# Low halves of the weights made by adding DMAs instead of the vector engine, in a two-layer decoder kernel

## The chip, the cores and the metric

The kernel runs on one core of a Trainium2 chip. The metric is the device time of one launch in microseconds. The engines are named as in the profile: PE multiplies matrices, PEld loads its weights, DVE is the vector engine, ACT the scalar engine, POOL is GpSimd, and SP issues DMAs.

## The reference

The program is one inference step of a trunk with two layers. 512 new prompt tokens and 8 x 4 sample tokens (544 in all, width 1024) go through it with the same weights:

```python
for l in range(DEPTH):                       # DEPTH = 2
    h = rms_norm(x, norm1_w[l])
    z = h @ w_in[l]                          # 1024 -> 3584: q, k, v, gate of retention; q, k, v of attention
    x = x + concat(retention(z), dilated_attention(z)) @ w_out[l]     # 1024 -> 1024
    h = rms_norm(x, norm2_w[l])
    u = h @ w_up[l]                          # 1024 -> 5632
    c = causal_depthwise_conv3(u)            # with a bias
    x = x + (silu(c[:, :2816]) * c[:, 2816:]) @ w_down[l]             # 2816 -> 1024
y = rms_norm(x, final_norm_w)
```

The sample tokens attend to 1024 cached positions and carry a retention state and a convolution buffer; the new keys, values, states and buffers are outputs too. All data are float32.

## The kernel before, in words

**Products in three passes.** A float32 product is made of three products of the PE's faster float32r type. Each operand is split into a high half (the operand rounded to float32r) and a low half (the operand minus its high half). `products` (lines 1368 to 1374) adds up high x high, high x low and low x high in that order; the third pass is the first that reads the weight's low half. The 544 tokens are two column groups of 272, so one 128 x 128 piece of a weight costs six matmuls.

**Blocks and units.** `main` is the list of output blocks in the order of the work: per layer 28 of `w_in`, 16 of `w_out` (four row pieces each), 44 of `w_up`, and 16 of `w_down`. Their weights come in units (`halves`), mostly 512 KB (128 partitions x 1024 numbers, 48 matmuls); the last eight blocks of `w_down` have units of 256 KB (24 matmuls). `load_w` (line 321) issues a unit's load on SP's queue into `raw`. `split_w` (line 335) lets ACT write the high half `wh` from `raw`, and spawns a piece of work that lets DVE write the low half `wl` = `raw` - `wh`. `raw`, `wh` and `wl` have three buffers each (`UNITS`). In the main loop (lines 1400 to 1419) the load of unit s+3 is issued at the start of unit s, and unit s+2 is split in the middle of unit s.

**What sets the order.** The program is written out once, by hand and by a planner: `Clock` (line 66) keeps a modelled time for every engine, for one DMA queue and for every tile; `Engine.charge` adds the modelled cost of each instruction. Between the matmuls of the main blocks `Stream.pump` takes up waiting pieces (attention, retention, evacuations, convolutions, splits), when their inputs are ready by the model; `st.before` does so while the PE would wait for an operand. So each engine has one fixed queue, and an instruction that waits holds up all behind it.

**Stages of a layer.** The `w_in` blocks run with attention and retention woven in; then `w_out`; then `w_up`, with convolution, gating and (class `Weave`) most of `w_down` woven in as a seven-product scheme, whose sums of weights (`sums`) and of activations (`fa`, `fb`) POOL makes; then the rest of `w_down`, which ends in the last eight blocks of 24 matmuls. After each of these eight, ACT and DVE prepare the next norm (`xh`, `sq`, `xl`). POOL issues no DMA in this kernel.

Of the kernel before, what the change touches and what calls it, by code (L numbers as in the profile page):

```python
# [9 lines left out]
F32 = mybir.dt.float32  # L10
F32R = mybir.dt.float32r
AF = mybir.ActivationFunctionType
OP = mybir.AluOpType
# [8 lines left out]
KB = D // 128  # L22
# [24 lines left out]
NCONV = 352  # L47
EARLY = 640
UNITS = 3


SEM = {"pe": 0.22, "act": 0.2, "dve": 0.14, "pool": 0.08, "sp": 0.1}
# [2 lines left out]
def need(kind, *aps, banks=0):  # L55
    return kind, aps, banks


def free_size(ap):
    n = 1  # L60
    for d in ap.shape[1:]:
        n *= d
    return n
# [36 lines left out]
class Engine:  # L100
# [20 lines left out]
    def charge(self, method, outs, ins, args, kw):  # L121
        c, kind = self.clock, self.kind
        n = free_size(outs[0]) if outs else 0
        if method == "dma_start":
            c.now["sp"] = max(c.now["sp"], c.when("sp", ins)) + 0.06
            c.dma = max(c.dma, c.now["sp"] + 0.8) + n * outs[0].shape[0] * 4 / 3.6e5
            c.wrote[c.key(outs[0])] = ("sp", c.dma + 1.0)
            return
        if kind == "pe":
            rows = outs[0].shape[0]  # L130
            if method == "transpose":
                cost = max(n, 128) * 2 / 2400
            elif (kw["lhsT"]).dtype == F32R:
                cost = max(n / 2400, 0.107)
            else:
                side = min(rows, kw["lhsT"].shape[0])
                cost = max(n * 4 / 2400, 0.21) / (1 if side > 64 else 128 // side)
            cost += 0.003
        elif kind == "act":
            ptr = sum(free_size(i) == 1 for i in ins[1:])  # L140
            cost = 1.3 if method.startswith("preload") else n / 1200 + 0.093 * (1 + ptr)
        elif kind == "dve":
            half = method in ("tensor_scalar", "tensor_copy")
            cost = (n * (0.5 if half else 1) + 66 + (60 if len(ins) > 2 else 0)) / 960
        else:
            cost = 0.1 + n * (2.2 if len(ins) > 1 else 1.0) / 1000
        c.issue(kind, outs, ins, cost)
# [84 lines left out]
def trunk(ctx: ExitStack, tc: tile.TileContext, xin, w_in, w_out, w_up, w_down, q_down, kc, vc, s0, sctx_d, params_d,  # L232
# [3 lines left out]
    pe, act, dve, pool, sp = (Engine(clock, k, e) for k, e in (  # L236
        ("pe", nc.tensor), ("act", nc.scalar), ("dve", nc.vector), ("pool", nc.gpsimd), ("sp", nc.sync)))
# [7 lines left out]
    st = Stream(clock, SHARE)  # L245
    uid = [0]

    def name(s):
        uid[0] += 1
        return f"{s}_{uid[0]}"  # L250

    def blk(shape, dt=F32, s="b"):
        return work.tile(shape, dt, name=name(s), tag="blk", bufs=NBLK)
# [8 lines left out]
    def EW(eng, *aps):  # L262
        return need(eng, *aps)
# [20 lines left out]
    def rotate(t, tag, bufs):  # L284
        ends = rot.setdefault(tag, [])
        if len(ends) >= bufs:
            old = clock.key(ends[len(ends) - bufs])
            last = max(clock.used.get(old, ("pe", 0.0)), clock.wrote.get(old, ("pe", 0.0)), key=lambda v: v[1])
            clock.used[clock.key(t)] = last
        ends.append(t)  # L290
        return t
# [12 lines left out]
    main = []  # L304
    halves = []
# [12 lines left out]

    raw, split = {}, {}

    def load_w(s):
        if s < len(halves):
            i, a, b = halves[s]
            if s < 4:
                raw[s] = blk([128, b - a, 128], F32, "raw")
            else:
                raw[s] = rotate(wpool.tile([128, b - a, 128], F32, name=name("raw"), tag="raw", bufs=UNITS), "raw",
                                UNITS)
            if main[i]["count"] > 1:
                sp.dma_start(raw[s].rearrange("p (n k) c -> p n k c", n=main[i]["count"]),  # L330
                             main[i]["src"].rearrange("n p k c -> p n k c"))
            else:
                sp.dma_start(raw[s], main[i]["src"][:, a:b, :])

    def split_w(s, at_once=False):
        if s < len(halves):
            i, a, b = halves[s]
            if s < 4 or i >= len(main) - KB:
                hi, lo = (blk([128, b - a, 128], F32R, n) for n in ("wh", "wl"))
            else:  # L340
                hi, lo = (rotate(wpool.tile([128, b - a, 128], F32R, name=name(n), tag=n, bufs=UNITS), n, UNITS)
                          for n in ("wh", "wl"))
            w = raw.pop(s)
            act.activation(hi, w, AF.Copy)

            def rest():
                dve.tensor_sub(lo, w, hi.bitcast(F32))
                split[s] = (hi, lo)
                return
                yield  # L350
            if at_once:
                list(rest())
            else:
                st.spawn(rest(), "split", EW("dve", hi))

# [976 lines left out]
    for l in range(DEPTH):  # L1332
        mixer(l)
        ffn(l)


    first = norms[0][0]
    act.preload_act_table_set("natural_log_exp_and_others")
# [11 lines left out]
    for what, n in start:  # L1350
        if what == "x":
            sp.dma_start(x[n], xin[:, n])
        else:
            load_w(n)
    load_w(4)
    for what, n in start:
        if what == "x":
            list(first.scale(n))
            if n < 4:
                list(first.square(n, pool))  # L1360
        else:
            split_w(n, True)
# [17 lines left out]
    for k in range(KB):  # L1380
        if k == 2:
            load_w(5)
        if k == 4:
            split_w(4)
            load_w(6)
        if k == 6:
            split_w(5)
        for n in range(2):
            s = 2 * n + k // 4
            products(main[n], ps[n], k, parts_of(s), k // 4 * 4)  # L1390
            if k % 4 == 3:
                split.pop(s)
            if k == KB - 1:
                main[n]["evac"](ps[n])
                ps[n] = None
            st.pump(0.7)
# [3 lines left out]
    for i, b in enumerate(main[2:-KB]):  # L1400
# [4 lines left out]
        for pi, (a, e) in enumerate(b["parts"]):  # L1405
            s = b["first"] + pi
            at, count = b["at"], b["count"]
# [16 lines left out]
    for c in range(2):  # L1424
        for n, b in enumerate(main[-KB:]):
            s, nk = b["first"], b["nk"]
# [145 lines left out]
```

## Time and profile before

| | before |
|---|---|
| median of three runs | 1441.15 us (1440.74 to 1441.16) |
| profiled execution | 1442.15 us, its span 1440.4 us |
| PE busy | 1404.5 us, 98% of the span |
| PEld busy | 1331.5 us, 92% |
| DVE busy | 1066.9 us, 74% |
| ACT busy | 582.4 us, 40% |
| POOL busy | 411.8 us, 29% |
| DMA, share of 16 engines | 34.4% by SP's queue, 172.01 MB |

Busy time is time in which an engine executed something. A PE that is 98% busy is not at its peak everywhere, since matmuls overlap in its pipeline; the number of matmuls in a stretch says more. A wait says what ended an engine's idle time. Every operation goes through one helper, so all lines are L118, and the tiles' names tell the operations apart.

### The profile page before, as it was taken

To read this page: it belongs to the slowest core of one execution; us is meant where nothing else is said; L and a number is where in the kernel's file an instruction comes from. 1 tells how busy PE (TensorE), PEld (TensorE's weight loads), DVE (VectorE), ACT (ScalarE), POOL (GpSimd) and SP (SyncE) were. 2 spreads that over 40 slices of the span, in tenths; PEclk is the share of its full clock that TensorE was granted. 3 is DMA by queue.
4 is the path that set the end of the run, shared out by engine and by line. 5 is a ranking of instruction groups with operands and counts; after the bars stand their busy time and mean duration, and the time that the engine had idled before them with its cause. 6 is when DMAs were issued, how large, how long until landed. Compare 5 with 4: busy or idle time off the path is not lost.

```text
span 1440.4 us, 28487 instructions
## 1 busy us (share of the span) xinstructions
PE 1404.5 (98%) x11442; PEld 1331.5 (92%) x11442; DVE 1066.9 (74%) x1911; ACT 582.4 (40%) x986; POOL 411.8 (29%) x745
## 2 busy tenths in 40 slices
PE   8999999999999999999999999999999999999997
PEld 8888888999999999999997888799999999999996
DVE  8767545687888888887777764455978797979775
ACT  4344323444434343433524442333544343434334
POOL 4312222002334454530021221110024353535303
PEclk9999999999999999999999999999999999999999
DMA  6214683433322222222332238732433222222222
GB/s 237 98 60 155 249 299 118 139 115 126 103 88 95 83 103 76 101 75 67 109 110 83 89 142 289 283 129 91 147 111 101 77 103 89 89 89 89 74 63 85
DMA packets 70821, 173.84 MB, mean 121 GB/s; under 512 B 7584, under 2 KB 11808, under 8 KB 70688
## 3 DMA queue, kind: packets, MB, share of 16 engines
q1 hardware_dynamic: 70688, 172.01, 34.4%
q8 instruction: 90, 1.47, 0.4%
q14 instruction: 43, 0.35, 0.1%
HBM read 159.77 MB, written 12.21 MB: 119 GB/s over the span
## 4 chain that ended last, share of the span: by engine, by line
PE 74%; DVE 16%; POOL 4%; issue 3%; ACT 2%; DMA 1%; SPq 0%; DVEq 0%; ACTq 0%; POOLq 0%
PE ps L118 52%; PE sec L118 22%; DVE p L118 3%; DVE rb L118 3%; DVE c L118 2%; DVE wl L118 2%; DVE y L118 1%; POOL sums L118 1%; POOL fb L118 1%; DVE u L118 1%; POOL fa L118 1%; ACT c L118 1%; DVE x L118 1%; DVE ra L118 1%; DVE fl L118 1%
## 5 line engine op out<-in xcount | busy, mean ns | idle before, releaser
L118 PE MATMUL ps<-xh,wh 128*128 128x272 f32 x2304 | 488.7, 293 | 1.9 <-ACT wh L118 1.6
L118 PE MATMUL ps<-xh,wl 128*128 128x272 f32 x2304 | 476.6, 288 | 1.4 <-DVE wl L118 1.3
L118 PE MATMUL ps<-xl,wh 128*128 128x272 f32 x2304 | 476.9, 288 | 0.0
L118 PEld LDWEIGHTS ps<-xh,wh 128*128 128x128 f32 x2304 | 360.2, 189 | 19.9 <-issue 15.5
L118 PEld LDWEIGHTS ps<-xh,wl 128*128 128x128 f32 x2304 | 361.7, 188 | 1.8 <-DVE wl L118 1.8
L118 PEld LDWEIGHTS ps<-xl,wh 128*128 128x128 f32 x2304 | 361.7, 188 | 0.1
L118 DVE TENSOR_TENSOR wl<-raw,wh 128x1024 fp32r<-128x1024 f32 (+1 forms) x182 | 220.3, 1211 | 14.8 <-ACT wh L118 13.5
L118 ACT ACTIVATE wh<-raw 128x1024 fp32r<-128x1024 f32 (+1 forms) x182 | 182.0, 1001 | 67.8 <-PE ps L118 59.0
L118 ACT ACTIVATE c<-u,taps 128x560 f32<-128x560 f32 x88 | 75.4, 857 | 279.5 <-DVE u L118 197.3
L118 DVE SCALAR_TENSOR_TENSOR c<-u,taps,c 128x560 f32<-128x560 f32 x176 | 150.6, 855 | 47.9 <-ACT c L118 44.2
L118 POOL COPY last<-u 128x2 f32<-128x2 f32 (+1 forms) x176 | 50.2, 317 | 344.3 <-DVE u L118 336.4
L118 DVE TENSOR_TENSOR x<-x,sec 128x272 f32<-128x272 f32 (+1 forms) x224 | 105.1, 472 | 44.0 <-PE sec L118 42.5
L118 POOL TENSOR_TENSOR sums<-uraw 128x256 f32<-128x256 f32 x64 | 69.1, 1080 | 84.7 <-DVE sl L118 84.6
L118 DVE TENSOR_TENSOR u<-ps,rstd 128x512 f32<-128x512 f32 (+1 forms) x176 | 68.9, 432 | 13.1 <-PE ps L118 12.7
L118 DVE TENSOR_TENSOR rb<-ps,rope 32x544 f32<-32x544 f32 (+1 forms) x96 | 69.2, 721 | 1.4
L118 DVE TENSOR_TENSOR x<-x,ps 128x544 f32<-128x544 f32 (+1 forms) x72 | 46.9, 654 | 30.8 <-PE ps L118 30.7
L118 DVE CUSTOM_DVE_ANT_0 p<-sec,cst 128x128 f32<-128x128 f32 (+3 forms) x64 | 29.2, 489 | 53.3 <-PE sec L118 53.1
L118 PE MATMUL sec<-fh,sh 128*128 128x272 f32 x192 | 56.3, 293 | 8.1 <-DVE x L118 8.1
L118 POOL TENSOR_TENSOR kr<-ra,rb 128x512 f32<-128x512 f32 (+1 forms) x16 | 14.1, 904 | 151.2 <-DVE rb L118 113.0
L118 PE MATMUL sec<-fl,sh 128*128 128x272 f32 x192 | 55.3, 288 | 0.0
L118 PE MATMUL sec<-fh,sl 128*128 128x272 f32 x192 | 55.3, 288 | 0.0
L118 PE MATMUL ps<-ch,wh 128*128 128x272 f32 x256 | 53.5, 290 | 0.0
(194 smaller groups left out, 2388.4 us busy)
## 6 DMA issues: line engine op xcount, KB each, us to landing
raw<-w_up SPq DMA_DIRECT2D x88, 512.0 KB, 3.3
raw<-w_in SPq DMA_DIRECT2D x54, 512.0 KB, 4.0
kt<-kc SPq DMA_DIRECT2D x80, 256.0 KB, 5.8
vt<-vc SPq DMA_DIRECT2D x80, 256.0 KB, 5.3
uraw<-q_down SPq DMA_DIRECT2D x32, 512.0 KB, 3.8
raw<-w_out SPq DMA_DIRECT2D x16, 512.0 KB, 3.7
s<-s SPq DMA_DIRECT2D x16, 256.0 KB, 6.9
sret_o<-s SPq DMA_DIRECT2D x16, 256.0 KB, 2.4
```

Source lines behind the costliest of these rows:

```text
L118: return f(*args, **kw)
```

## The change

For the blocks in `added` (all but the first three and the last eight of `main`) the low half is made in another way. ACT writes the negated high half into `wl`, and POOL then issues a DMA that reads the same weights from HBM a second time and adds them to what stands in `wl`. DVE has no part in it. `raw` is then read by one ACT instruction alone. The planner is told that such a DMA takes POOL 1.0 us and the modelled DMA queue twice as long as a plain one.

```diff
+def ADDED(block):
+    return True
@@ Engine.charge
+        if method == "dma_start" and kind == "pool":
+            c.issue(kind, [], [*outs, *ins], 1.0)
+            c.dma = max(c.dma, c.now["pool"] + 1.0) + n * outs[0].shape[0] * 4 / 1.8e5
+            c.wrote[c.key(outs[0])] = ("sp", c.dma + 1.0)
+            return
@@ trunk
+    added = set()
+
+    def weights_of(s, t):
+        i, a, b = halves[s]
+        n = main[i]["count"]
+        if n > 1:
+            return t.rearrange("p (n k) c -> p n k c", n=n), main[i]["src"].rearrange("n p k c -> p n k c")
+        return t, main[i]["src"][:, a:b, :]
@@ load_w
-            if main[i]["count"] > 1:
-                sp.dma_start(raw[s].rearrange("p (n k) c -> p n k c", n=main[i]["count"]),
-                             main[i]["src"].rearrange("n p k c -> p n k c"))
-            else:
-                sp.dma_start(raw[s], main[i]["src"][:, a:b, :])
+            sp.dma_start(*weights_of(s, raw[s]))
@@ split_w
+            def add():
+
+                act.activation(lo, hi.bitcast(F32), AF.Copy, scale=-1.0)
+                yield EW("pool", lo)
+                pool.dma_start(*weights_of(s, lo), accum_op=OP.add)
+                split[s] = (hi, lo)
             if at_once:
                 list(rest())
+            elif i in added:
+                st.spawn(add(), "split", EW("act", hi))
             else:
                 st.spawn(rest(), "split", EW("dve", hi))
@@ after the layers' blocks are listed
+    added.update(i for i, b in enumerate(main) if 2 < i < len(main) - KB and ADDED(b))
```

## Rows read from the trace of the kernel before

**Rows 1.** Busy time of each engine, from the page.
```profile
PE 1404.5 (98%) x11442; PEld 1331.5 (92%) x11442; DVE 1066.9 (74%) x1911; ACT 582.4 (40%) x986; POOL 411.8 (29%) x745
```

**Rows 2.** What PE waited for: us in total, times, longest us.
```profile
PE sec L118 <- DVE x L118: 8.1, 10, 1.6
PE sec L118 <- DVE p L118: 6.9, 8, 1.1
PE sec L118 <- DVE fl L118: 2.8, 6, 1.1
...
PE sec L118 <- DVE pm L118: 1.3, 4, 0.4
```

**Rows 3.** The chain of waits, in time: start us, us, what.
```profile
330.90 43.58 PE ps L118 x348
376.36 3.67 POOL sums L118 x3
380.03 1.82 POOL fa L118
```

**Rows 4.** Stretches: us, busy us (instructions) of PE, PEld, DVE, ACT, POOL; PEclk, DMA share, GB/s.
```profile
290.00:376.00 86.00, 86.00 (x678) 85.48 (x677) 69.48 (x102) 38.62 (x50) 9.53 (x37) 1.00 0.36 121
376.00:660.00 284.00, 278.34 (x2204) 276.44 (x2204) 239.80 (x383) 113.41 (x159) 127.76 (x218) 1.00 0.26 88
```

**Rows 5.** The splits by shape: instructions, busy us, mean ns, idle before them.
```profile
L118 DVE TENSOR_TENSOR wl<-raw,wh 128x1024 fp32r<-128x1024 f32 x162 | 204.7, 1263 | 14.2 <-ACT wh L118 12.9
L118 ACT ACTIVATE wh<-raw 128x1024 fp32r<-128x1024 f32 x162 | 169.7, 1047 | 61.4 <-PE ps L118 59.0 <-DMA raw<-w_in 0.9 <-ACT sq L118 0.7
...
L118 DVE TENSOR_TENSOR wl<-raw,wh 128x512 fp32r<-128x512 f32 x20 | 15.7, 789 | 0.6 <-ACT wh L118 0.6
...
L118 ACT ACTIVATE wh<-raw 128x512 fp32r<-128x512 f32 x20 | 12.3, 622 | 6.4 <-issue 5.6 <-DMA raw<-w_in 0.3 <-DMA raw<-w_down 0.3
```

**Rows 6.** Stretches again, for instructions that touch wl alone (PE, PEld, DVE).
```profile
144.00:216.00 72.00, 21.09 (x102) 15.96 (x102) 7.33 (x6) 1.00 0.78 274
864.00:936.00 72.00, 21.06 (x102) 15.99 (x102) 7.34 (x6) 1.00 0.81 285
376.00:660.00 284.00, 105.29 (x510) 80.03 (x510) 40.97 (x32) 1.00 0.26 88
```

**Rows 7.** DMA: SP's queue, and issues with KB each and median us to landing.
```profile
q1 hardware_dynamic: 70688, 172.01, 34.4%
...
raw<-w_up SPq DMA_DIRECT2D x88, 512.0 KB, 3.3
...
raw<-w_down SPq DMA_DIRECT2D x16, 256.0 KB, 2.6
```

**Rows 8.** The tile raw: its loads' issue in ns, and their time to landing.
```profile
L118 SPq DMA_DIRECT2D raw<-w_up x88: 327/328/947, 306.1 to 1354.3; - x88
...
DMA to landing us min/median/max: 2.5/3.4/7.4
```

**Rows 9.** POOL's sums: count, ns min/median/max; then their mean in ns.
```profile
L118 POOL TENSOR_TENSOR sums<-uraw x64: 728/744/2237, 375.5 to 1346.4; 128x256 f32<-128x256 f32 x64
...
L118 POOL TENSOR_TENSOR sums<-uraw 128x256 f32<-128x256 f32 x64 | 69.1, 1080 | 84.7 <-DVE sl L118 84.6
```

**Rows 10.** ACT in the last eight blocks of layer 0: start us, us, instruction.
```profile
699.86 0.75 ACT L118 ACTIVATE xh<-x,par 128x544 fp32r<-128x544 f32 x1 [2.03 <-DVE x L118]
700.52 0.64 ACT L118 ACTIVATE sq<-x 128x544 f32<-128x544 f32 x1
701.07 0.62 ACT L118 ACTIVATE wh<-raw 128x512 fp32r<-128x512 f32 x1
...
707.92 0.63 ACT L118 ACTIVATE wh<-raw 128x512 fp32r<-128x512 f32 x1 [0.16 <-ACT wh L118]
...
713.94 1.06 ACT L118 ACTIVATE wh<-raw 128x1024 fp32r<-128x1024 f32 x1 [0.23 <-ACT wh L118]
```

**Rows 11.** DVE there: block 0's result is added at 699.11.
```profile
699.11 0.72 DVE L118 TENSOR_TENSOR x<-x,ps 128x544 f32<-128x544 f32 x1 [1.68 <-PE ps L118]
```

**Rows 12.** ACT's splits in the stretch where w_up begins.
```profile
327.24 1.05 ACT L118 ACTIVATE wh<-raw 128x1024 fp32r<-128x1024 f32 x1
336.15 1.04 ACT L118 ACTIVATE wh<-raw 128x1024 fp32r<-128x1024 f32 x1
...
352.13 1.04 ACT L118 ACTIVATE wh<-raw 128x1024 fp32r<-128x1024 f32 x1
360.74 1.04 ACT L118 ACTIVATE wh<-raw 128x1024 fp32r<-128x1024 f32 x1
```

**Rows 13.** What ACT and POOL waited for.
```profile
POOL last L118 <- DVE u L118: 336.4, 66, 10.1
ACT c L118 <- DVE u L118: 197.3, 66, 5.6
```

## The prediction

> **What bounds the kernel now.** I read the engines' busy times first, then what PE waited for, then the chain of waits and the stretches, and only then the splits and the DMAs. The busy times show PE at 98% [rows 1], so DVE's 74% is no bound in itself. The chain shows the pace at which PE is full: 348 matmuls in 43.58 us, 0.125 us each [rows 3]. A 512 KB unit of 48 matmuls is then 6.01 us, a unit of 24 is 3.01 us. From 290 to 376 us PE does 678 matmuls in 86 us, which is that pace. From 376 to 660 us it does 2204 in 284 us, where the pace would allow 2268: some 8 us are lost in this stretch, and DVE is 84% busy in it [rows 4]. PE's own waits say on whom: on DVE for x, p, fl and pm, together 8.1 + 6.9 + 2.8 + 1.3 = 19.1 us over the whole span [rows 2]. More than 19.1 us cannot be had from relieving DVE, unless the order of the work changes for other reasons. The chain also passes through POOL's sums and forms at the head of a woven group [rows 3].
>
> **The change, part by part.** It touches 161 units of 512 KB (of 162) and 8 of 256 KB (of 20).
>
> *DVE.* It loses 161 x 1.263 + 8 x 0.789 = 210 us [rows 5], a fifth of its work; from 376 to 660 us it loses 41.0 of 239.8 us [rows 4, 6]. The worth is that part of PE's 19.1 us that goes with it. A wait for x or fl is 0.7 us on the average (10.9 us in 16 times), less than one split, so it is gone wherever one split stands ahead of the awaited instruction in DVE's queue. With a split for every 8.9 us (284/32) [rows 6] I count half of the waits: -5.5. For p and pm, where splits come every 12 us, a quarter of 8.2: -2. I take **-7**; ends 0 (the freed time turns into idle time of DVE) and -19.1.
>
> *ACT.* It gains 161 x 1.047 + 8 x 0.622 = 174 us; the negation has the shape of the high half, whose row I use [rows 5]. That makes 756 us, 52% of the span, in time that ACT now spends idle.
>
> *POOL.* It gains 169 DMA issues. No row shows one. The ends are SP's issue of 0.33 us [rows 8] and the longest of POOL's sums, 2.24 us; I take the mean of such a sum, 1.08 us, as the nearest instruction of that queue [rows 9]: 183 us, or 41% for POOL. POOL's 336.4 us of idle time before `last` [rows 13] hide it; behind the waiting issue stand `sums`, `fa` and `fb`, on which DVE and then PE wait. I cost this at 0. If the cover is gone at the eight woven groups' heads, where the chain does run through POOL [rows 3], it is 8 x 1.08 = +8.6; the other end is 0.
>
> *The way to the low half.* Now it is one ACT and one DVE instruction. After the change it is ACT, ACT, POOL's issue, and a DMA. No row shows an adding DMA. A plain 512 KB load lands 3.3 us after its issue [rows 7]. SP's queue moves 172.01 MB in 34.4% of 1440.4 us, 347 GB/s, so 512 KB take 1.5 us of the 16 engines. The adding DMA must also read what stands in `wl`; I count its bytes twice: 3.3 + 1.5 = 4.8 us. The ends are the plain 3.3 us and 7.4 us, the slowest plain load [rows 8], plus the 1.5: 8.9 us; I take 4.8, since most stretches have the DMA engines a third busy or less, as where the 3.3 was measured. In all 1.05 + 1.05 + 1.08 + 4.8 = **8.0 us** for 512 KB, and 0.62 + 0.62 + 1.08 + (2.6 + 0.75) = **5.7 us** for 256 KB. The unit is split in the middle of the unit two before it, and PE first needs the low half at the fifth matmul, 0.5 us on. So there is room for 1.5 x 6.01 + 0.5 = 9.5 us, or 1.5 x 3.01 + 0.5 = 5.0 us.
>
> The Trainium skill ("DMA: Bandwidth & Descriptors", Anatomy of one DMA) gives a DMA issued from GpSimd some 2.0 us plus its bytes at 436 GB/s. By that an estimate for 512 KB counted twice is 4.4 us in place of 4.8, and the sum below would be some 2 us lower; no row here shows such a DMA.
>
> *Where the room is too small.* (a) The last eight blocks of layer 0 are 24 matmuls each, and PE has nothing else there. Block 0 ends at about 699.0 us, where its sum is added [rows 11], so the middle of block 1 is at 700.5; ACT begins the split belonging to it at 701.07, behind `xh` and `sq` [rows 10], 0.6 us late. The room is 4.4 us against 5.7; a lack of 1.3 us for every 1.5 blocks lengthens each by 0.8 us, over blocks 2 to 7 by 5; a split that comes early, as at 707.92, takes some of it: +4. The first unit of layer 1 has 512 KB: its split begins at 713.94 [rows 10], block 7 ends at 699.0 + 7 x 3.01 = 720.1, the room is 6.7 us against 8.0: +1. Together **+5**; ends 0, and with a landing of 8.1 us (10.5 in all) (10.5 - 4.4)/1.5 = 4.1, 1.1 us per block above 3.01, +6 for the blocks, and 12.1 - 6.7, +5, for the first unit: +11.
> (b) In unwoven stretches the margin is 9.5 - 8.0 = 1.5 us. ACT's splits should come every 6 us, and two from 327 to 361 us come 8.9 and 8.6 us after the one before [rows 12], 2.9 and 2.6 late: 1.4 + 1.1 beyond the margin, 5 in two layers. ACT is late there for waiting on DVE (197.3 us before `c` [rows 13]), which shrinks: **+2**; ends 0 and +5.
> (c) DMA traffic: 86.5 MB of adding DMAs, counted twice, are 498 us of the 16 engines, 35% more beside 34.4%. It matters where the cached keys and values are loaded: the share is 0.78 and 0.81 of 72 us, with six splits in each [rows 6]. That is 56.2 + 6 x 3.0 = 74.2 us and 58.3 + 18 = 76.3 us in 72: 2.2 and 4.3 us too much. Part of the loads can slide: **+4**; ends 0 (bytes counted once) and +6.5.
> Elsewhere a unit takes 8.9 us or more, the room is 13 us, and the longer way is hidden behind PE's own products.
>
> *Sum:* -7 + 0 + 5 + 2 + 4 = +4, on the profiled execution's 1442.15 us: 1446.15. That execution was 1.0 us above the median of 1441.15, so **1445 us**.
>
> **The rivals.**
> *Faster: the adding DMA lands like a plain one.* Its place is the wait for the low half: with 3.3 and 2.6 us the ways are 6.5 and 4.9 us, (b) and (c) vanish and (a) is 0.5 of lack per 1.5 blocks, +2. It decides once the landing is under 3.5 us. Then DVE's relief stands nearly alone, and where all of x and fl and 3 us of p go with it: -14 + 2 on 1442.15, less 1.0: 1429. For it: DVE is 84% busy where PE loses its 8 us. Against it: an addition needs two operands.
> The Trainium skill ("SBUF — State Buffer", Who interferes with whom) says that a VectorE instruction with two SBUF inputs contends with a GpSimd instruction that reads SBUF; a split is such a one, and POOL's sums take 728 ns at best and 1080 on the average [rows 9], which agrees. By that rule this rival gains some weight, since 169 such instructions go.
>
> *No difference.* The relief is worth as much as (a) costs: PE's waits for x come out of the woven scheme itself (its next product must not be written before DVE has read the last), so only 2 us go, and (a) to (c) are 2 us: 1441. For it: PE at 98%.
>
> *A slow adding ring.* The landing is 8.9 us. The way for 512 KB is 12.1 us, and an unwoven unit takes (12.1 - 0.5)/1.5 = 7.7 us in place of 6.0. The stretch from 290 to 376 us alone has 14 units [rows 4], in two layers 28: +48. With (a) +11, (c) +6.5 and -7: 1442.15 + 58.5 - 1.0 = 1500. It decides as soon as landing takes over 6.3 us. For it: nothing shows that the DMA engines add at the pace at which they copy. Against it: PE's woven stretches still cover it.
>
> *The change doesn't do what it says:* if the adding DMAs waited for each other on POOL, POOL's queue would hold up the sums; that is the slow ring's case with the loss in the woven stretches, counted there.
>
> **How the numbers follow.** The forecast (1444 to 1460) has 0.36, the faster rival 0.34, no difference 0.15, the slow ring 0.15. About 3 us, 0.2%, is what a measurement of this kernel tells from no change. So faster 0.34, same 0.15, slower 0.51. The forecast's own range is 1444 to 1460. The whole range takes in the faster rival almost to its time and part of the way to the slow ring: 1430 to 1475; 0.08 is left below and 0.1 above.
>
> **What would show it.** DVE busy near 857 us, ACT near 756, POOL near 595; a queue of POOL's own with some 86 MB. The landing of the adding DMAs decides: under 3.5 us the faster rival, 4 to 6 the forecast, over 6.3 the slow ring. Step (a) is right if the last eight blocks of layer 0 take about 4 us longer and PE waits there for a DMA into `wl`; (b) if such waits stand at the head of `w_up`; (c) if PE waits for `kt` or `vt`, or attention ends later. The relief is right if PE's waits for DVE x and fl are halved. The prediction is wrong if PE waits for `wl` in the woven stretches, where I cost the longer way at nothing.

## The result, and the profile after the change

The changed kernel takes 1464.6 us (median of 4 runs, 1461.72 to 1465.67), the kernel before 1441.16 us beside it. The ratio is 1.016, 95% interval 1.0142 to 1.0177: 23.4 us slower, where +4 was forecast. The profiled execution took 1465.67 us, its span is 1463.9 us. The direction was as forecast, the size six times as large.

The busy times of the engines (busy us, share of the span, instructions), which answer to [rows 1]:

```profile
PE 1417.5 (97%) x11442; PEld 1338.3 (91%) x11442; DVE 875.8 (60%) x1742; ACT 749.8 (51%) x1155; POOL 494.7 (34%) x914
```

DVE has lost 191 us, ACT gained 167, POOL 83. The work moved as planned; PE has the same 11442 matmuls, and yet 13.0 us more of busy time. What PE waited for (us in total, times, longest) shows both sides of the trade, against [rows 2]:

```profile
PE ps L123 <- DMA wl<-w_up: 11.6, 11, 1.6
PE ps L123 <- DMA wl<-w_down: 6.8, 4, 4.5
PE sec L123 <- DVE p L123: 3.2, 5, 0.7
PE sec L123 <- DVE pm L123: 2.7, 4, 0.9
...
PE sec L123 <- DVE x L123: 1.3, 4, 0.4
PE ps L123 <- DMA wl<-w_in: 1.2, 2, 0.7
PE sec L123 <- DMA kt<-kc: 1.2, 1, 1.2
...
PE sec L123 <- DVE al L123: 0.8, 3, 0.3
```

The waits on DVE that [rows 2] list (19.1 us) are down to 7.2: `fl` is gone, `x` fell from 8.1 to 1.3. In their place stand 19.6 us of waits for the DMA of the low half, which the kernel before does not have. The sum of all PE waits went from 25.1 to 34.4 us, +9.3, and PE's busy time rose by 13.0: together 22.3 of the 23.5 us by which the span grew. So more than half of the loss shows not as waiting but as longer busy time of PE; part of that is the clock (granted 0.997 in the mean before, 0.992 after; 0.005 of 1464 us is 7).

The DMA part (queue: packets, MB, share of 16 engines; then issues, KB each, median us to landing), against [rows 7]:

```profile
q0 software_dynamic: 27920, 86.52, 33.8%
q1 hardware_dynamic: 70688, 172.01, 33.6%
...
raw<-w_up SPq DMA_DIRECT2D x88, 512.0 KB, 4.3
wl<-w_up POOLq DMA_DIRECT2D x88, 512.0 KB, 5.3
raw<-w_in SPq DMA_DIRECT2D x54, 512.0 KB, 6.3
wl<-w_in POOLq DMA_DIRECT2D x53, 512.0 KB, 7.8
kt<-kc SPq DMA_DIRECT2D x80, 256.0 KB, 8.2
```

Half the bytes of SP's queue take as large a share of the 16 engines as all of SP's: 33.8% for 86.52 MB, 33.6% for 172.01 MB. The transfers beside them got slower too: `raw<-w_up` lands after 4.3 us instead of 3.3, the cached keys after 8.2 instead of 5.8.

The two stretches of [rows 4] after the change (us, busy us and instructions of PE, PEld, DVE, ACT, POOL; PEclk, DMA share, GB/s):

```profile
290.00:376.00 86.00, 85.86 (x674) 85.11 (x674) 56.59 (x95) 55.36 (x68) 19.84 (x45) 1.00 0.77 193
376.00:660.00 284.00, 276.55 (x2172) 274.17 (x2172) 201.27 (x348) 143.96 (x189) 131.12 (x252) 0.99 0.60 147
```

The first keeps its pace within 4 matmuls, half a microsecond. The second is the one that was to gain: DVE is relieved from 239.8 to 201 us, and PE still does 2172 matmuls where it did 2204.

Where the time went can be read by laying the two executions over each other, unit by unit: when does PE start the first matmul of the same unit? The changed kernel is behind by 2.4 us at the start of layer 0's `w_up` (at 325 us before), 6.6 at its end (683), 6.2 at the first of the last eight blocks (696), 18.1 at the second unit of layer 1 (727), 18.5 at the start of its `w_up` (1033) and 22.6 at its end (1390). So the end of layer 0 costs 11.9 us in this execution, the two stretches of `w_up` 4.2 + 4.1 = 8.3, layer 0's attention 2.4. The matmul numbers 5600 and 6000 in the expectation of experiment 1 stand for the end of `w_up` and the end of layer 0.

**A woven group's head.** In time (start us, us, engine, instruction, idle before it and what ended it), one of the eleven places where PE waits for `wl<-w_up`:

```profile
602.84 1.05 ACT L123 ACTIVATE wh<-raw 128x1024 fp32r<-128x1024 f32 x1
...
603.50 1.28 POOL L123 TENSOR_TENSOR fb<-y,y 128x272 f32<-128x272 f32 x1
...
604.74 1.25 POOL L123 TENSOR_TENSOR fb<-y,fa 128x272 f32<-128x272 f32 x1
...
604.89 1.05 ACT L123 ACTIVATE wl<-wh 128x1024 fp32r<-128x1024 f32 x1
...
605.95 0.94 POOL L123 TENSOR_TENSOR sums<-uraw 128x256 f32<-128x256 f32 x1
...
606.96 1.10 POOL L123 TENSOR_TENSOR sums<-sums,uraw 128x256 f32<-128x256 f32 x1
...
608.72 0.87 POOL L123 DMA_DIRECT2D wl<-w_up  x1 [0.23 <-issue]
...
613.91 0.52 PE L123 MATMUL ps<-xh,wl 128*128 128x272 f32 x2 [1.53 <-DMA wl<-w_up]
```

ACT has written the negated high half at 605.94. POOL issues the adding DMA at 608.72, 2.8 us later: it is still at the forms `fb`, the sums and some small copies, which the program handed to it first. The DMA lands 5.1 us later, and PE has waited 1.53 us.

PE was ready for this low half at 612.38, 9.5 us after its split began at 602.84. That is the room here, and not the 13 us that the prediction took for woven stretches. Its 8.9 us per unit are a mean: in the kernel before, of the eight units from 446.0 to 516.3 us two take 6.0 us, one 6.8, and five 9.8 to 10.9. At this same place the kernel before had even less room between split and use, 6.5 us:

```profile
600.15 1.05 ACT L118 ACTIVATE wh<-raw 128x1024 fp32r<-128x1024 f32 x1
...
606.66 0.42 PE L118 MATMUL ps<-xh,wl 128*128 128x272 f32 x2
```

Of the eleven waits for `wl<-w_up`, seven with 9.7 us stand at such heads. At six of them the DMA was issued 2.8 to 3.4 us after the negation's end, as here; at the seventh (462.60) it was issued at once and took 7.2 us to land. The other four, 1.9 us, stand earlier in `w_up`, where every unit takes some 6 us.

**The end of layer 0.** The last blocks of `w_down`, 24 matmuls each:

```profile
713.03 0.52 PE L123 MATMUL ps<-yh,wl 128*128 128x272 f32 x2 [1.25 <-DMA wl<-w_down]
713.91 7.89 SPq L123 DMA_DIRECT2D raw<-w_in  x3
...
720.16 0.52 PE L123 MATMUL ps<-yh,wl 128*128 128x272 f32 x2 [0.82 <-DMA wl<-w_down]
721.85 0.93 SPq L123 DMA_DIRECT2D rope<-rope  x2
722.41 0.86 POOL L123 DMA_DIRECT2D wl<-w_down  x1 [2.16 <-ACT wl L123]
...
723.71 0.52 PE L123 MATMUL ps<-yh,wl 128*128 128x272 f32 x2 [0.27 <-DMA wl<-w_down]
...
731.49 0.82 PE L123 MATMUL ps<-yh,wl 128*128 128x272 f32 x2 [4.49 <-DMA wl<-w_down]
```

Three blocks wait 0.3 to 1.3 us each, and then the last waits 4.49 us: its 256 KB, issued at 722.41, land 9.0 us later, while SP's queue has loads of the next layer under way. After that wait PE is slow. The stretches (columns as above, PEclk before the DMA share):

```profile
724.00:730.00 6.00, 3.00 (x24) 2.78 (x23) 3.56 (x5) 5.73 (x8) 1.82 (x2) 0.97 1.00 285
730.00:736.00 6.00, 4.51 (x20) 4.52 (x21) 0.00 (x0) 0.62 (x1) 0.86 (x1) 0.50 1.04 244
```

The granted clock is 0.50, the lower of TensorE's two levels (1.2 GHz), and 20 matmuls take 4.51 us, 0.226 each in place of 0.125 [rows 3]: about 2 us lost after the wait is over. The DMA engines are full in both stretches (1.00 and 1.04).

### The profile page after: what moved, and what is told of

It is laid out like the page before. It is cut to its first block, busy times and chain, and to the rows that moved or that the text cites. A ratio compares the mean times of both kernels' runs of the same rounds, so it can differ in the third digit from the quotient of the medians.

```text
span 1463.9 us, 28760 instructions
## 1 busy us (share of the span) xinstructions
PE 1417.5 (97%) x11442; PEld 1338.3 (91%) x11442; DVE 875.8 (60%) x1742; ACT 749.8 (51%) x1155; POOL 494.7 (34%) x914
## 3 DMA queue, kind: packets, MB, share of 16 engines
q0 software_dynamic: 27920, 86.52, 33.8%
q1 hardware_dynamic: 70688, 172.01, 33.6%
## 4 chain that ended last, share of the span: by engine, by line
PE 75%; DVE 8%; POOL 5%; issue 5%; DMA 4%; ACT 3%; SPq 0%; DVEq 0%; ACTq 0%; POOLq 0%
PE ps L123 53%; PE sec L123 22%; DVE c L123 2%; DVE rb L123 2%; DMA wl<-w_up 2%; POOL sums L123 1%; DVE p L123 1%; POOL fb L123 1%; POOL wl L123 1%; DMA wl<-w_in 1%; DMA kt<-kc 1%; POOL fa L123 1%; ACT c L123 1%; POOL sq L123 1%; DMA wl<-w_down 1%
## 5 line engine op out<-in xcount | busy, mean ns | idle before, releaser
L123 PEld LDWEIGHTS ps<-xh,wh 128*128 128x128 f32 x2304 | 361.2, 189 | 22.9 <-issue 19.7
L123 PEld LDWEIGHTS ps<-xh,wl 128*128 128x128 f32 x2304 | 361.8, 189 | 18.5 <-DMA wl<-w_up 14.8
L123 ACT ACTIVATE wh<-raw 128x1024 fp32r<-128x1024 f32 (+1 forms) x182 | 182.0, 1000 | 31.9 <-PE ps L123 30.3
L123 DVE SCALAR_TENSOR_TENSOR c<-u,taps,c 128x560 f32<-128x560 f32 x176 | 154.1, 876 | 63.3 <-ACT c L123 60.0
L123 ACT ACTIVATE wl<-wh 128x1024 fp32r<-128x1024 f32 (+1 forms) x169 | 175.2, 1037 | 4.0
L123 POOL DMA_DIRECT2D wl<-w_up x88 | 76.0, 864 | 222.4 <-ACT wl L123 218.9
L123 POOL DMA_DIRECT2D wl<-w_in x53 | 46.0, 868 | 227.4 <-ACT wl L123 164.9
L123 POOL TENSOR_TENSOR sums<-uraw 128x256 f32<-128x256 f32 x64 | 57.7, 901 | 78.9 <-DVE sl L123 68.9
L123 POOL COPY last<-u 128x2 f32<-128x2 f32 (+1 forms) x176 | 38.1, 265 | 120.2 <-DVE u L123 120.2
L123 DVE TENSOR_TENSOR ra<-ps,rope 128x544 f32<-128x544 f32 x32 | 23.1, 722 | 75.4 <-PE ps L123 75.2
```

Of the source, the lines that this page charges most:

```text
L123: return f(*args, **kw)
```

## The experiments

The theory to test was A: the low half comes late at two kinds of place, the end of layer 0 (too little room, then a slow landing) and the woven heads (POOL's issue behind its own work), and the second operand of the adding DMA is what makes the way too long. The rivals said that one place carries all of it, that the DMAs' mere traffic does it, or that the order of the work has changed. In the diffs `ADDED` is asked with the number of a block, counted through both layers (104 each); blocks for which it says no keep DVE's subtraction. Times are medians, with the interval of the ratio to the kernel before, which was 1441.3 to 1441.5 us beside each.

**1. Without the end of layer 0.**
```
-    return True
+    return not 96 <= block < 106
```


> DVE makes the low half again in ten blocks alone: the last eight of layer 0 (24 matmuls each) and the first two of layer 1. Theory A (single places where the low half comes too late; the trace shows 11.4 us lost between the matmuls 5600 and 6000, some 7 of them by one DMA into wl that took 9 us to land while rope tables and w_in loads shared the engines, and by PE's clock being at its lower level after that wait): about 1453 us, PE's waits for wl<-w_down gone and no stretch of low clock near 730 us. Theory B (the added traffic slows everything in proportion, 23 us for 86.5 MB): 3.1 MB less, so 1 us less, 1463 us.

1456.11 us, ratio 1.0098 [1.0083, 1.0114]: 8.5 us less than the changed kernel. PE's waits for `w_down` are gone, those for `w_up` stay (13.6 us, 12 times). The end carries over a third of the loss, and not all.

**2. Only `w_up`.**
```
-    return True
+    return 44 <= block % 104 < 88
```


> Adding DMAs in the 88 blocks of w_up alone (46.1 MB of 86.5). Theory A: what is lost is what the trace shows between the start of w_up and its end, 4.0 us in layer 0 and 3.6 in layer 1: about 1449 us. Theory B: 46.1/86.5 of 23.4, 12.5 us: 1453.5 us. A third theory (DVE's relief in w_up is worth more than the late low halves there, and the rest of the change hides it): under 1441 us.

1449.95 us, 1.0066 [1.0049, 1.0083]: +8.6 us. DVE's relief is all there (PE's wait for `x` is 1.0 us in place of 8.1, `fl` gone) and yet this part loses. PE waits for `wl` 12.6 us in 12 times. Six of these, 9.7 us, stand at the heads of woven groups, at 467.33 for 1.71 us, at 538.68 for 1.61, at 610.14 for 1.71, and as regularly in layer 1; the rest stands earlier in `w_up`.

**3. An earlier split.** The split of the unit after next at the start of a unit, not in its middle: half a unit more of room.
```
-                if 2 * (at * (e - a) + k - a) == count * (e - a):
+                if at == 0 and k == a:
```


> All blocks as in the changed kernel, but unit s+2 is split at the start of unit s and not in its middle, so the adding DMA has half a unit more (3 us, in the last eight blocks 1.5 us). Theory A: most waits for wl go (19.6 us of PE's idle time in the changed kernel), 1448 to 1454 us. Theory B: no change, 1462 to 1466 us.

1488.32 us, 1.0324 [1.0309, 1.034]: 24 us worse, against every expectation. What ACT waited for (us in total, times, longest) says why:

```profile
ACT wh L123 <- PE ps L123: 111.1, 40, 6.3
```

In the changed kernel this wait is 30.3 us in 12 times. The buffer for the high half is still being read by PE at the earlier moment, so ACT stands at the head of its queue and everything behind it is late; PE waits for `wl<-w_up` 20.6 us. More room was not to be had by this earlier start, with three buffers.

**4. POOL's copies of `last` out of the way.** They are handed out later, as work of their own.
```
-            pool.tensor_copy(F.last[s][:, j, 0:2], u[:, 512:514])
...
+            st.spawn(keep(F.last[s][:, j], u), "ffn", EW("pool", u))
```


> All blocks as in the changed kernel, but POOL's two copies into last are written out only when the planner takes u to be done, so that an adding DMA no longer stands behind copies that wait for DVE (in the changed kernel a quarter of the 169 DMAs go out more than 1.6 us after the negation has ended, up to 4.5). Theory A with POOL's queue as the cause in w_up: waits for wl<-w_up (11.6 us) fall below 4, 1456 to 1460 us. If the late landing in w_up comes from the DMA engines, not from POOL's queue: no change, 1463 to 1466 us.

1463.9 us, 1.0157 [1.0142, 1.0172]: no change. Three quarters of the DMAs are now issued within 0.31 us of the negation's end (1.6 us before this edit), but those at the woven heads are not: PE waits 15.8 us in 8 times, at six of the heads 2.4 to 2.8 us each. It is not `last` that they stand behind, but the forms and the sums.

**5. Without the late blocks.** The six blocks per layer at which PE waited, and the end, keep DVE.
```
-    return True
+    return not 96 <= block < 106 and block % 104 not in (52, 55, 62, 63, 71, 79)
```


> As e1 (DVE again makes the low half in the last eight blocks of layer 0 and the first two of layer 1), and in each layer also in the six w_up blocks before whose low half PE waited in the changed kernel: once per woven group, where the adding DMA stands on POOL's queue behind a run of fa, fb and sums. Theory A (single places): e1's 1456.1 us less the 13.6 us of waits for wl<-w_up that are left in it, 1443 to 1446 us, with waits for wl<-w_up under 3 us. Rival (the planner's new order makes other blocks late instead): 1452 us or more, the waits at other blocks.

1459.34 us, 1.0126 [1.0111, 1.0141]: 3 us more than without the end alone (1), as the rival had it. PE now waits at other blocks (2.28 us at 548.95, 2.33 at 623.15, and the same in layer 1), and a wait for DVE's `al` has come up, 5.6 us. The program plans its order by its own clock; where six blocks change, the order changes, and the lateness moves on to the next blocks at a head.

**6. Only the end of layer 0.** Eight units of 256 KB and two of 512 KB, 3.1 MB in all.
```
-    return True
+    return 96 <= block < 106
```


> Adding DMAs in the ten blocks around the end of layer 0 alone, 3.1 MB of 86.5. Theory A: the loss of that place alone, 8 to 11 us: 1449 to 1453 us. Theory B (traffic in proportion): 1442 us.

1451.52 us, 1.0077 [1.0062, 1.0092]: +10.2 us from ten DMAs. In the profiled execution, which took 1455.19 us, PE's waits for `wl<-w_down` are 8.2 us in 5 times, the longest 5.24 at 725.64; the last 256 KB land 10.0 us after their issue at 715.59.

**7. Only `w_in` and `w_out`.**
```
-    return True
+    return block % 104 < 44 and block not in (104, 105)
```


> Adding DMAs in the w_in and w_out blocks of both layers alone (without the first two of layer 1), 35 MB. Theory A: what the trace of e1 shows lost there: some 2 to 5 us in layer 0 and about 1 in layer 1, where DMAs are busiest: 1444 to 1447 us. Theory B: 35/86.5 of 23.4, 9.5 us: 1451 us.

1445.43 us, 1.0028 [1.0016, 1.0039]: +4.2 us. PE waits 1.9 us for the cached keys; the DMA share from 180 to 216 us is 0.98, against 0.86 in the kernel before. The three parts add up: 10.2 + 8.6 + 4.2 = 23.0 of 23.4 us.

**8. The same DMAs without the addition.** Every instruction in the same place, but POOL's DMA only copies the weights over the negated high half. This leaves out the addition.
```
-                pool.dma_start(*weights_of(s, lo), accum_op=OP.add)
+                pool.dma_start(*weights_of(s, lo))
```


> All blocks as in the changed kernel, but POOL's DMA copies the weights into wl and does not add them to what stands there (the negated high part is overwritten; the low half is then not the low half). The order of all instructions is the same. If reading the second operand is what makes the DMAs late, they land about 1.5 us earlier (w_up 5.3 to under 4 us), the queue's share falls from 33.8% to about 17%, and most waits for wl go: 1448 to 1454 us. If POOL's queue and the other loads on the ring set the time: landing at 4.5 us or more, 1460 to 1465 us.

1446.66 us, 1.0039 [1.0025, 1.0053]: 18 of the 23.4 us are gone. The DMA part, in the columns above:

```profile
q0 software_dynamic: 27920, 86.52, 19.7%
...
wl<-w_up POOLq DMA_DIRECT2D x88, 512.0 KB, 4.0
...
wl<-w_in POOLq DMA_DIRECT2D x53, 512.0 KB, 5.3
```

The same packets and bytes take 19.7% in place of 33.8%, 1.7 times less, and land 1.3 to 2.5 us earlier. POOL's issue is shorter too: 0.55 us on the average for `w_up` in place of 0.86. The page "Collectives: The Full Stack" of the Trainium skill (Part 3) says that an addition in the DMA engines needs two reads for one write; the ratio of 1.7 agrees with that, short of 2.

What PE waits for is told as much by this run as its time:

```profile
PE sec L123 <- DVE al L123: 8.6, 8, 1.2
PE sec L123 <- DVE p L123: 4.5, 6, 1.0
PE sec L123 <- DVE pm L123: 2.7, 4, 0.9
PE ps L123 <- DMA wl<-w_down: 2.3, 3, 1.7
```

No wait for `wl<-w_up` is left. But DVE is relieved here as fully as in the changed kernel (872 us busy), and PE's waits on DVE are not down to 7.2 us: `al`, the low part of the woven weights, for which PE did not wait in the kernel before, takes 8.6. Laid over the kernel before in the same way, this run gains 1.9 us over `w_up` of layer 0 and 1.2 over that of layer 1. That is what the relief is worth there when no low half of `w_up` is late: about 3 us, where the prediction counted 5.5. The end of layer 0 loses 5.3 us, about all that this run is slower by.

**9. The issue first.** POOL's DMA issue goes into its queue right behind the negation, ahead of forms and sums that are handed out later.
```
                 act.activation(lo, hi.bitcast(F32), AF.Copy, scale=-1.0)
-                yield EW("pool", lo)
                 pool.dma_start(*weights_of(s, lo), accum_op=OP.add)
...
```


> The changed kernel, but POOL's DMA issue is put into POOL's queue right behind ACT's negation, ahead of any forms and sums that are handed out later; POOL then waits for the negation at the head of its queue. Theory A (in the woven stretches the issue is late because it stands behind POOL's forms and sums): the waits of PE for wl<-w_up, 11.6 us, mostly go, and with them their half-pace clock: 1456 us (1452 to 1459). Rival B (the landing itself, or the stop of POOL's queue behind the waiting issue, is what costs): the forms and sums come late instead, PE waits for DVE's fl or POOL's sums: 1465 us or more.

1464.27 us, 1.0158 [1.0141, 1.0175]: no change in all, so theory A's 1456 is refuted for the whole kernel; it is within 1 us of rival B's 1465, but the waits that came up are not the `fl` and sums that B named. PE's waits (us in total, times, longest):

```profile
PE ps L123 <- DMA wl<-w_up: 7.5, 4, 2.2
PE sec L123 <- DVE al L123: 6.8, 4, 1.8
PE ps L123 <- DMA wl<-w_down: 4.9, 3, 2.4
PE ps L123 <- DMA wl<-w_in: 3.6, 3, 2.3
```

The heads of the later woven groups no longer wait for `wl`: the four waits left stand at 383 and 404 us and their like in layer 1, where `w_up` is not yet fully woven. In their place PE waits for `al`, and longer for `w_in` (2.29 us at 48.40). That POOL's queue, which now stops at a waiting issue, is what makes these late is argued and not shown; but what the order gave in one place was paid in others.

**10. The same for `w_up` alone.**
```
-    return True
+    return 44 <= block % 104 < 88
...
-                yield EW("pool", lo)
```


> Only the 88 blocks of w_up go through adding DMAs, with the issue right behind the negation in POOL's queue. Without that order the part alone cost +8.6 us. Theory A: the waits for wl<-w_up go (12.6 us), DVE's relief stays (its x waits are 1.0 in place of 8.1 us): 1438 us (1434 to 1442), at or under the kernel before. Rival B: 1450 us as without it.

1447.08 us, 1.004 [1.0025, 1.0055]: +5.6 in place of +8.6 us, between the two theories. The waits, beside which `x` no longer appears:

```profile
PE sec L123 <- DVE p L123: 6.9, 8, 1.1
PE sec L123 <- DVE al L123: 6.8, 4, 1.8
PE ps L123 <- DMA wl<-w_up: 6.5, 4, 2.2
```

At the heads of the woven groups no wait for `wl` is left, and that order was worth about 3 us. The rest stays: two units per layer earlier in `w_up`, blocks 52 and 55 (376.74 and 398.18 us), and `al`. At 557.83 PE waits 1.78 us for `al`: DVE starts it at 556.83, behind 2.13 us of the convolution's `c`. At such a place the time that DVE saves on splits is taken by what the program now puts in front.

**11. The end of layer 0 without its last three blocks.**
```
-    return True
+    return 96 <= block < 103
```


> Of the end of layer 0 only blocks 96 to 102, the first seven of w_down's last eight, go through adding DMAs; the last one and the first two blocks of layer 1 do not. With all ten the part cost +10.2 us. Theory A (it is the one DMA of the last block, landing 9 us after its issue behind the next layer's loads, and the slow clock after it): +3 us, 1444 us (1442.5 to 1446). Rival B (the prediction's chain, a lack in each of the eight blocks): +7 us or more, 1448 to 1450 us.

1445.5 us, 1.0029 [1.0017, 1.0041]: +4.0 us, against +10.2 with all ten. What PE waited for, and the landing times of the tile `wl` (one answer each):

```profile
PE ps L123 <- DMA wl<-w_down: 3.3, 3, 1.2
```
```profile
DMA to landing us min/median/max: 4.0/4.3/5.6
```

So the seven blocks cost about 4 us by the chain that the prediction describes, and the last block with the first two of layer 1 cost the other 6.

**12. Only the woven blocks, the issue first.** The combination that the others point to: `w_up` from block 59 on.
```
-    return True
+    return 59 <= block % 104 < 88
...
-                yield EW("pool", lo)
```


> Only blocks 59 to 87 of each layer, the woven ones of w_up, go through adding DMAs, with the issue right behind the negation in POOL's queue; the blocks at the head of w_up, where a unit takes 6 us and PE waited 6.5 us for wl<-w_up at 376.74, 398.18, 1087.92 and 1108.22 us, keep DVE's subtraction. Theory A (the way to the low half costs only where the room is 9.5 us; in the woven stretches it is covered once the issue stands first): those waits go, DVE's x waits stay near 1 us, 1440 us (1437 to 1443), within 0.2% of the kernel before or a little under. Rival B (the new order of the work costs what DVE's relief gives, as with the al waits of 6.8 us): 1446 us or more.

1443.31 us (11 runs) against 1441.32 (15), 1.0017 [1.0008, 1.0026]: 2 us slower, and 0.3 us above theory A's range. It is within A's 0.2% and far from rival B's 1446, but not at or under the kernel before. PE's waits:

```profile
PE sec L123 <- DVE p L123: 6.9, 8, 1.1
PE sec L123 <- DVE al L123: 6.8, 4, 1.8
PE sec L123 <- DVE x L123: 4.0, 4, 1.4
...
PE sec L123 <- DVE pm L123: 1.3, 4, 0.4
...
PE ps L123 <- DMA wl<-w_up: 0.3, 1, 0.3
```

The waits for `wl` are gone (0.3 us). The waits on DVE are 6.9 + 6.8 + 4.0 + 1.3 = 19.0 us, against 19.1 in [rows 2]: with 65 us less on DVE, PE waits on it as long. `p` and `pm` lie in attention, and the 4.0 us of `x` at the head of `w_up`, both of which this run leaves alone. In the woven stretches the other 6.9 us of `x` and `fl` are gone, and 6.8 us of `al` have come, the thing that rival B named. No version tried beats the kernel before.

## Why the prediction was right in its sign and wrong in its size

- **What moved.** DVE 857 us forecast, 875.8 measured; ACT 756 and 749.8; POOL 595 and 494.7. POOL is the one that is far off: the forecast added 183 us of issues to 411.8. The 169 issues took 153 (0.86 us each for `w_up`, 1.19 for `w_out`), but POOL's other work got 70 us shorter; its sums fell from 1080 ns on the average [rows 9] to 901.
- **DVE's relief, -7.** The waits named fell by 11.9 us, more than was counted, and yet the worth over `w_up` was some 3 us (experiment 8), where -5.5 was counted, with `al` late in their place. In experiment 12 the sum of the waits did not move at all. That a wait goes where a split stood ahead of the awaited instruction held for each tile and not for the sum: the order is planned anew, and another tile is late. The other -2 was for `p` and `pm`, whose waits all stand in attention.
- **POOL at 0, "hidden": the step that failed.** The longer way was costed at nothing in the woven stretches, from "a unit takes 8.9 us or more, the room is 13 us", and the prediction's last sentence said that it would be wrong if PE waited for `wl` there. It did, seven times, 9.7 us. Two things were missed. First, the 8.9 us are a mean, and at the heads, where units of 6.0 us follow each other, the room is 9.5 us. Second, the price is not the issue's length of 0.86 us but the order in the queues: at 613.91 the way was 3.1 us to the end of the negation (2.1 forecast), 2.8 us behind POOL's forms and sums (nothing forecast) and 5.1 us of landing, 11.0 us in all. The forecast's way of 8.0 us would have fitted even there. With the issue first (experiment 10) these waits go and 3 us come back; with a plain DMA (8) they go too. Together with the smaller relief, `w_up` cost +8.6 where the terms -5.5, 0 and +2 gave -3.5: 12.1 of the 19.4 us by which the forecast missed. The bound for a lost cover, 8 x 1.08 = +8.6, has the same size by chance; it priced POOL's issues, and not their place in the queue.
- **The way to the low half.** The landing was 5.3 us for `w_up`, where 4.8 was taken (bytes counted twice), and 7.2 and 7.8 for `w_out` and `w_in`. The forecast's own test, "4 to 6 us", held for `w_up`. Counting the bytes twice was right: 35% forecast, 33.8% measured. The Trainium skill's 2.0 us plus bytes at 436 GB/s ("DMA: Bandwidth & Descriptors", Anatomy of one DMA) gives an estimate of 4.4 us for twice the bytes; it came out 0.9 us short of the 5.3.
- **(a) The end of layer 0, +5.** Measured +10.2, near the bound of +11. The chain of seven blocks was well sized (4.0 against +4). The rest was forecast at +1 and cost 6: the bound with 8.1 us of landing came true for one DMA, 9.0 us where the median is 4.2 for this size, and the half-pace clock behind the wait (about 2 us) was in no term. What slows this DMA is only argued: the DMA engines are full there, with loads of `w_in` and the rotary tables in flight, and no run took these away alone. The addition seems to have a part in it: the plain DMA of the same block in experiment 8 landed after 5.1 us.
- **(b) Late splits in unwoven stretches, +2.** Next to nothing: from the start of layer 0's `w_up` to 374 us before the lag grows from 2.4 to 2.6 us. The sign that was named did come, four waits for `wl` early in `w_up`, 1.9 us in both layers; but the lag is 3.0 us behind them in layer 0, and 18.8 after 18.5 in layer 1, so little of it was lost.
- **(c) Traffic in the attention, +4.** The whole part of `w_in` and `w_out` measured +4.2 (experiment 7), what the relief of `p` and `pm` gives there included: the share from 180 to 216 us rose to 0.98, and in the changed kernel the cached keys land 2.4 us later. Little of it shows as PE's waits (1.9 us for the keys); PE's busy time is 6.9 us longer in that run. That the traffic costs it was not tested by itself; but where layer 0's `w_up` begins experiment 7 is 3.8 us behind the kernel before, and experiment 8, whose DMAs move the same bytes in 1.7 times less of the engines' time, 0.3 us.
- **The rivals.** The faster one was to decide by a landing under 3.5 us. No run had one: experiment 8 has plain DMAs at 4.0 us and is still 5.4 us slower than before, with some 3 us of relief where the rival counted 14. The slow ring was to decide by a landing over 6.3 us: `w_in` and `w_out` passed that, but not `w_up` in its unwoven stretch, on which its price rested.
- **The range.** 1464.6 us lies above the forecast's own range (1444 to 1460). That it lies in the whole range, 1430 to 1475, is luck: that part was left for the slow ring, and the ring's price did not come.

## What to carry to other kernels

An operation that moves from a compute engine to a DMA brings three things into the way to its result: the place in the queue of the engine that issues it, a landing of 4 to 8 us, and more load on the engines that bring the operands; measure the room at each consumer, not by a stretch's mean (8.9 us here hid units of 6.0), and look there for what already stands in the issuing queue. Relief of a busy engine is worth what its consumer waits for after the work has been ordered anew, so add up all waits on the engine, not the ones that you expect to vanish. And look behind a wait of a few us on PE for slower matmuls (here about 2 us after 4.49 us).

## What the runs showed of the hardware

- An adding DMA from POOL's queue takes 1.7 times the DMA engines' time of a copying one (33.8% against 19.7% of the span for 86.52 MB) and 0.86 us of POOL against 0.55 for the issue; both issues cost more than SP's 0.33 us [rows 8].
- A wait of PE can be followed by slower matmuls: after 4.49 us of waiting, at a granted clock of 0.50, 20 matmuls took 0.226 us each. Of the seven waits at the woven heads in the changed kernel, 0.98 to 1.55 us each, two were followed by a clock of 0.50 (from 542 and from 1194 us), the others by 1.00.
- The DMA of 256 KB for the last block of layer 0 took 9.0 us to land in the changed kernel and 10.0 in experiment 6, with the DMA engines full (1.00 in the changed kernel), where others of its size took a median of 4.2.
- POOL's sums took 17% less (1080 to 901 ns on the average) once DVE had lost 169 instructions with two inputs. With the splits of `w_up` left to DVE (experiment 7) they took 1074 ns, with these alone gone (2) 881. That agrees with the Trainium skill ("SBUF — State Buffer", Who interferes with whom), by which a VectorE instruction with two SBUF inputs contends with a GpSimd instruction that reads SBUF.
